# Moving three small pieces of work on VectorE and ScalarE in a gated MLP whose TensorE is nearly always busy

## The chip, the cores and the metric

The kernel runs on one core of a Trainium2 chip. The metric is the device time of one execution in microseconds (us); most executions of one kernel agree within 0.3%. Compared runs are fast ones (no lowered clock).

In the profile PE is TensorE (matmuls; PEld its weight loads), DVE is VectorE, ACT is ScalarE, POOL is GpSimd and SP issues most DMA transfers. L266 is line 266 of the kernel. Lines after 266 shift by some lines in the changed kernel: L270 becomes L276, L352 and L357 become L365 and L370, L320 becomes L333, L363 becomes L376, L347 becomes L360, L567 and L568 become L580 and L581.

## The reference

```python
# x: 16 x 256 x 512, w1: 512 x 4096, w2: 2048 x 512, all float32
h = x @ w1
gate, value = np.split(h, 2, axis=-1)
h = np.maximum(gate, 0) * value
return (h @ w2).astype(np.float32)
```

## The kernel before

The 4096 rows are done in four sets (s = 0 to 3) of 1024 rows. Both matrix products use a scheme with seven half-size products (P1 to P7) in place of eight, at the price of sums around them: sums of x ("x sums", S1 to S4), sums of weights (T1 to T4), and sums of the results in PSUM. X, Y and W are the PSUM tiles that the products accumulate into; "gating" is the step max(gate, 0) times value, which writes g; cc, pu and o are SBUF tiles for the sums around it.

The first product runs in 16 blocks per set. A block takes seven time slots of two matmuls (128x512), and each block is interleaved with its neighbours by the table SLOT. P4 of a block comes four slots after its P7; three slots after that P4 comes the next block's P7. So in DVE's queue a block's second-half gating (L270, behind P4) stands right ahead of the next block's cc (L266, behind P7):

```python
SLOT = {"P1": 0, "P5": 1, "P2": 3, "P6": 4, "P3": 5, "P7": 9, "P4": 13}   # PERIOD = 7

class Block:
    ...
    def P6(self):
        self.mm("P6", self.Y, False)                       # TensorE accumulates into PSUM tile Y
        nc.scalar.activation(self.u2, self.Y, COPY, scale=GS)
    def P3(self):
        self.mm("P3", self.W, False)
        ...
        nc.vector.scalar_tensor_tensor(out=self.c12, in0=self.W, ..., in1=self.u2, ...)       # L260, "cc<-W"
        nc.vector.scalar_tensor_tensor(out=self.g[:, self.jb, :TH], in0=self.X, ..., in1=self.c12, ...)  # L261
    def P7(self):
        self.mm("P7", self.Y, False)
        nc.vector.scalar_tensor_tensor(out=self.c22, in0=self.Y, ..., in1=self.p5, ...)       # L266, "cc<-Y"
    def P4(self):
        self.mm("P4", self.Y, False)                       # may start only when L266 has read Y
        nc.vector.scalar_tensor_tensor(out=self.g[:, self.jb, TH:], in0=self.Y, ..., in1=self.c22, ...)  # L270
```

The second product runs in four pairs (t = 0 to 3) per set, each with P1 to P7 of eight matmuls (128x256), spread by a list ORDER; its last P4 is interleaved with the next set's first block. "Looks" are checks of the weights' size: one is a square with a running sum on ACT, 128x1024, L179.

```python
ORDER = ("... P4 0, P5 2, P4 1, P6 2, P3 2, P7 2, P1 3, P4 2, P5 3, P2 3, P6 3, P3 3, P7 3, P4 3")

class Pair:
    ...
    def P6(self):
        nc.scalar.activation(self.pu[:, 1], self.Y, COPY, scale=1 / GS)
        for _ in range(2 if self.s else 1):
            some_look()
    def P4(self):
        nc.scalar.activation(self.o[:, 1, :DO // 2], self.Y, COPY, scale=1 / GS)
        ...
        if self.s == 0 and self.t < 3:
            some_look()
```

At the end of set 0 DVE makes the four x sums for set 1 itself, placed by step numbers in the second product's stream:

```python
for u in (84, 90, 93, 96):
    job(u, lambda sums=sums: next(sums))
...
advance(stream, 112 - TAIL - 10, jobs)
```

The x of set 1 reaches SBUF on a long road: POOL's queue issues a DMA that casts it to 16 bits in DRAM (`CASTS = {(0, 11): 1, ...}`: set 1, issued at block 11 of set 0), and eight transposing DMAs on SP's queue bring it in.

Of the kernel before, what the change touches and what calls it, by code (L numbers as in the profile page):

```python
# [96 lines left out]
def fast_way(ctx, tc, x2, w1, w2, out2, flag):  # L97
# [11 lines left out]
    _, J = w1.shape  # L109
    H, DO = w2.shape  # L110
    NS = T // (2 * TH)
    NJ = H // P
# [41 lines left out]
    def x_tiles():  # L154

        o = {n: xpool.tile([P, 2, TH], F16, name=f"x_{n}", tag=f"x_{n}")
             for n in ("A11", "A12", "A22", "S1", "S2", "S3", "S4")}
        o["A21"] = o["S3"]
        return o

    def sums_of(o, eng=nc.vector):
        for n, i0, i1, op in (("S1", "A21", "A22", ADD), ("S2", "S1", "A11", SUB), ("S4", "A12", "S2", SUB),
                              ("S3", "A11", "A21", SUB)):
            yield eng.tensor_tensor(o[n], o[i0], o[i1], op=op)  # L164
# [24 lines left out]
    def load_x(s, o):  # L189

        for h in range(2):
            for e in range(4):
                nc.sync.dma_start(out=o[f"A{h + 1}{e // 2 + 1}"][:, e % 2],
                                  in_=x16[s][h * TH:(h + 1) * TH, e * P:(e + 1) * P], transpose=True)

    def load_rows(s, i):

        t = halfs.tile([P, 8, P], F16, name="xh", tag="xh")
        nc.sync.dma_start(out=t.rearrange("p (b q) c -> p b (q c)", b=2),
                          in_=x16[s][i * 2 * P:(i + 1) * 2 * P].rearrange("(b p) d -> p b d", p=P))  # L200
        return t
# [24 lines left out]
    class Block:  # L226
# [25 lines left out]
        def P6(self):  # L252
            self.mm("P6", self.Y, False)
            nc.scalar.activation(self.u2, self.Y, COPY, scale=GS)  # L254
# [9 lines left out]
        def P7(self):  # L264
            self.mm("P7", self.Y, False)
            nc.vector.scalar_tensor_tensor(out=self.c22, in0=self.Y, scalar=GS, in1=self.p5, op0=MULT, op1=ADD)  # L266

        def P4(self):
            self.mm("P4", self.Y, False)
            nc.vector.scalar_tensor_tensor(out=self.g[:, self.jb, TH:], in0=self.Y, scalar=0.0,  # L270
                                           in1=self.c22, op0=MAX, op1=MULT)

    class Plain:

# [26 lines left out]
    class Pair:  # L301
# [43 lines left out]

        def P6(self):
            nc.scalar.activation(self.pu[:, 1], self.Y, COPY, scale=1 / GS)  # L347
            for _ in range(2 if self.s else 1):
                some_look()

        def P3(self):
# [10 lines left out]
        def P4(self):  # L362
            nc.scalar.activation(self.o[:, 1, :DO // 2], self.Y, COPY, scale=1 / GS)  # L363
            self.send(1, slice(0, DO // 2 if self.end else DO))
            if self.s == 0 and self.t < 3:  # L365
                some_look()

    ORDER = ("P1 0, P1 1, P2 0, P2 1, P1 2, P5 0, P2 2, P6 0, P3 0, P7 0, P5 1, P6 1, P3 1, P7 1, P4 0, P5 2, P4 1, "
# [5 lines left out]
    def mm2_stream(s, pairs):  # L374
        for step in (LAST_ORDER if s == NS - 1 else ORDER if s else FIRST_ORDER).split(", "):
            name, t = step.split()  # L376
            yield from pairs[int(t)].product(name)
# [3 lines left out]
    def advance(stream, n, todo={}):  # L381

        for _ in range(n):
            if stream is None:
                return
            at = stream_at[stream] = stream_at.get(stream, -1) + 1
            for job in todo.get(at, ()):
                job()
            next(stream, 0)
# [11 lines left out]
    def prepare(i):  # L401
        jb, n, _ = wl[i]
        copies.extend((i, c) for c in w1_ops(jb, n, ws.pop(i)))
# [51 lines left out]
    first_half, second_half = (xo["A11"], xo["A12"]), (xo["A21"], xo["A22"])  # L455
# [25 lines left out]
    sums = sums_of(xo)  # L481
# [15 lines left out]
    def some_look():  # L497
        if looks:
            looks.pop(0)()
# [43 lines left out]
    for s in range(NS):  # L543
        if s not in g_set:
            g_set[s] = gpool.tile([P, NJ, 2 * TH], F16, name="g", tag="g")
        g = g_set[s]
        first = NPLAIN if s == 0 else 0
        blocks = {jb: Block(xo, g, jb) for jb in range(first, NJ)}
        plan = {jb * PERIOD + at: (jb, n) for jb in blocks for n, at in SLOT.items()}
        stream = None  # L550
        last = NJ * PERIOD
        todo = 3
        for at in range(first * PERIOD, (NJ - 1) * PERIOD + 14):
            if at == last - 7:
                pairs = [Pair(s, g, t) for t in range(NB // 2)]
                stream = mm2_stream(s, pairs)
            if at in plan:
                jb, n = plan[at]
                if s == 0 and n == "P5" and jb % 2 == 0:
                    todo += 1  # L560
                    if todo < len(wl):
                        prepare(todo)
                    if 5 <= todo < 9:
                        n2 = ("B11", "T3", "B22", "B21")[todo - 5]
                        nc.gpsimd.dma_start(out=vop[n2], in_=w2_v[(0, 0, 1, 1)[todo - 5], (0, 1, 1, 0)[todo - 5]])
                if (s, n, jb) == (0, "P7", 13):
                    nc.gpsimd.tensor_tensor(vop["T1"], vop["T3"], vop["B11"], op=SUB)  # L567
                    nc.gpsimd.tensor_tensor(vop["T2"], vop["B22"], vop["T1"], op=SUB)  # L568
                if n == "P1" and jb == (14 if s == 0 else 2) and s + 1 < NS:
                    xo_next = x_tiles()  # L570
                    load_x(s + 1, xo_next)
                if n == "P1" and s and jb in (0, 3 if s == NS - 1 else 6):
                    wanted = [LOOKX[s, j] for j in range(NJ) if (s, j) in LOOKX]
                    rows += [load_rows(*r) for r in (wanted[3:] if jb else wanted[:3])]
                if n == "P1" and (s, jb) in CASTS:
                    cast_x(CASTS[s, jb])
                if s and n == "P3" and jb in SUMS and s + 1 < NS:
                    if jb == SUMS[0]:
                        sums = sums_of(xo_next, nc.gpsimd)
                    next(sums)  # L580
                getattr(blocks[jb], n)()  # L581
                if s == 0 and (n, jb) == ("P1", NPLAIN):
                    plain[1].value()
                if s == 0 and (n, jb) == ("P5", NPLAIN):
                    next(sums)
                    plain[1].gate(1)
                if n in ("P6", "P7"):
                    copy_some(1)
                if s == 0 and n == "P7" and jb % 2:
                    fetch(jb // 2 + 5, nc.sync)  # L590
                if n == "P6" and (s, jb) in LOOKX:
                    look_x(*LOOKX[s, jb])
            elif at >= last - 7:
                advance(stream, 2)
            else:
                advance(prev, 2)
        jobs = {}

        def job(at, *what):
            jobs.setdefault(at, []).extend(what)  # L600

        for t, at in enumerate(SUMS_AT if s else SUMS_FIRST):
            sums = sums_of(pairs[t].op)
            for u in at:
                job(u, lambda sums=sums: next(sums))
        if s == 0:
            for n2, i0, i1, at in (("T3", "B22", "T3", (46, 50)), ("T4", "B21", "T2", (57, 58))):
                for i, u in enumerate(at):
                    part = [vop[n][:, i * NJ // 4:(i + 1) * NJ // 4] for n in (n2, i0, i1)]
                    job(u, lambda part=part: nc.vector.tensor_tensor(*part, op=SUB))  # L610
            for i, u in enumerate((74, 78, 82, 83)):
                job(u, lambda i=i: plain_w_end(0, NPLAIN, i))
        if s + 1 < NS:
            xo = xo_next
            if s == 0:
                sums = sums_of(xo)
                for u in (84, 90, 93, 96):
                    job(u, lambda sums=sums: next(sums))
            looks = [lambda i=i: LOOK_JOBS[i]() for i in range(8 * s, 8 * s + 8)]
            advance(stream, 112 - TAIL - 10, jobs)  # L620
        else:
            verdict = []
            job(18, lambda: verdict.append(judge()))
            job(46, lambda: count(verdict[0]))
            job(78, lambda: verdict.append(nc.values_load(
                flag[0:1, 0:1], min_val=0, max_val=1, skip_runtime_bounds_check_because="a comparison wrote it")))
            job(90, lambda: tc.mark_branch_hint_location("general", "LikelyTaken", [ENG.PE, ENG.DVE, ENG.SP]))
            advance(stream, 112, jobs)
        prev = stream
# [29 lines left out]
```

## Time and profile before

| | before |
|---|---|
| time, median of 3 runs | 313.85 us (313.25 to 314.24) |
| span of the profiled run | 311.5 us, of which TensorE's last matmul ends at 306.7 |
| granted TensorE clock | 1.000 |

The head of the page of the kernel before: busy time by engine.

```profile
span 311.5 us, 5217 instructions
...
PE 302.7 (97%) x1870; PEld 182.8 (59%) x1870; DVE 231.2 (74%) x378; ACT 177.9 (57%) x350; POOL 153.9 (49%) x186
```

97% looks as if nothing were left. The record of a pipelined matmul overlaps the next one's, however: a 128x512 matmul is recorded with 379 ns and the next starts after 216 ns. The record hides a short stall. So I used the time between the starts of neighbouring matmuls, less 213.3 ns per 512 columns, and call the rest a gap. The 213.3 ns are an estimate: one column a cycle at 2.4 GHz, the highest clock that the Trainium skill's "TensorE: Matmul & The Clock Gate" gives in its first table; the 215 to 216 ns from start to start in this trace lie close to it. In undisturbed stretches the gap is 2 to 3 ns. Sums of gaps are taken beyond 2.5 ns each. They come to some 9 us in the kernel before, nearly 4 of them in the first 10 us.

The waits of PE (engine and tile that waited, what it waited for, us in total, times, longest):

```profile
...
PE Y L233 <- DVE cc L266: 0.7, 2, 0.5
PE Y L320 <- DVE o L357: 0.6, 1, 0.6
PE X L233 <- ACT Y L240: 0.2, 1, 0.2
...
```

This view shows the large stalls only. The gaps before P4 of all blocks after the first sum to 1.60 us in the trace, 0.37 us of it in one place (47 us); most are 35 to 46 ns and 5 to 18 ns in alternation. The view reports two of the P4 waits: the one at 47 us and one of 0.5 us before the first block's P4. Its wait for ACT (L240) is one at 18 us, which the change does not touch; the two stalls of 0.29 us behind L240 at the ends of sets 1 and 2, shown below, are not in it.

One ordinary block in the timeline of the kernel before (start, duration, engine, line, what):

```profile
103.77 0.69 DVE L260 SCALAR_TENSOR_TENSOR cc<-W,pu 128x512 f32<-128x512 f32 x1 [0.44 <-ACT pu L254]
104.49 0.69 DVE L261 SCALAR_TENSOR_TENSOR g<-X,cc 128x512 f16<-128x512 f32 x1
...
105.10 0.68 DVE L270 SCALAR_TENSOR_TENSOR g<-Y,cc 128x512 f16<-128x512 f32 x1
...
105.70 0.68 DVE L266 SCALAR_TENSOR_TENSOR cc<-Y,pu 128x512 f32<-128x512 f32 x1
105.96 0.59 PE L233 MATMUL W<-x_S_687,w_B_89 128*128 128x512 f16 x2
...
106.43 0.59 PE L233 MATMUL Y<-x_A_683,w_T_93 128*128 128x512 f16 x2
```

L270 (the previous block's second half) runs ahead of L266. L266 ends at 106.38 and the P4 matmul starts at 106.43; at pace it would have started at 106.39.

The end of set 0 in the timeline of the kernel before. The x sums are L164, the output sums L352 and L357:

```profile
82.98 0.69 DVE L164 TENSOR_TENSOR x_S_684<-x_S_686,x_A_683 128x1024 f16<-128x1024 f16 x1 [2.14 <-DMA x_A_683<-x_598]
...
85.04 0.68 DVE L164 TENSOR_TENSOR x_S_686<-x_A_681,x_S_686 128x1024 f16<-128x1024 f16 x1
...
85.64 0.42 DVE L352 SCALAR_TENSOR_TENSOR o<-W,pu_1002 128x256 f32<-128x256 f32 x1
...
85.97 0.42 DVE L357 SCALAR_TENSOR_TENSOR o<-Y,pu_1002 128x256 f32<-128x256 f32 x1
...
86.44 0.60 PE L320 MATMUL Y<-v_T_100,g 128*128 128x256 f16 x4 [0.57 <-DVE o L357]
```

DVE does four x sums, then the two output sums; P4 of the last pair starts 0.74 us late.

The end of set 1 in the same view. Two squares (L179) hold ACT, so its copy L240 is late, and P2 of the next set's first block (x_A_1145) with it, by 0.29 us:

```profile
158.58 1.06 ACT L179 ACTIVATE sq<-w_T_90 128x1024 f16<-128x1024 f16 x1
...
159.63 0.58 ACT L240 COPY Y<-X 128x512 f32<-128x512 f32 x1
...
160.26 0.59 PE L233 MATMUL X<-x_A_1145,w_B_88 128*128 128x512 f16 x2
```

### The profile page before, as it was taken

How to read it: one execution, taken by the hardware profiler on the slowest of the kernel's cores; microseconds unless marked ns; L12 is line 12 of the kernel's file. 1: busy time of each engine (PE TensorE's matmuls, PEld its weight loads, DVE VectorE, ACT ScalarE, POOL GpSimd, SP SyncE). 2: the span in 40 equal slices, each digit the busy share in tenths (PEclk: the TensorE clock that was granted, in tenths of full speed). 3: DMA queues.
4: the chain of work that ended last, by engine and by line, in shares of the span. 5: the costliest groups of instructions: out<-in, count | busy, mean ns of one | idle time of the engine just before them, and what ended most of it. 6: DMA issues, size and time to landing. Idle time of an engine off the chain costs nothing.

```text
span 311.5 us, 5217 instructions
## 1 busy us (share of the span) xinstructions
PE 302.7 (97%) x1870; PEld 182.8 (59%) x1870; DVE 231.2 (74%) x378; ACT 177.9 (57%) x350; POOL 153.9 (49%) x186
## 2 busy tenths in 40 slices
PE   7999999999999999999999999999999999999993
PEld 3934444588844444478864444458884444448883
DVE  1598888889758888887527888888536888888841
ACT  2688885445855555537675555545776555553230
POOL 2199999920058999400028889700007998700000
PEclk9999999999999999999999999999999999999999
DMA  7978695999784233000355400000335110000132
GB/s 241 354 221 258 183 222 76 202 205 151 214 243 102 70 69 67 2 0 36 136 171 117 117 1 3 0 0 9 128 107 164 37 34 1 0 3 0 69 140 66
DMA packets 37340, 32.87 MB, mean 106 GB/s; under 512 B 14400, under 2 KB 32320, under 8 KB 37184
## 3 DMA queue, kind: packets, MB, share of 16 engines
q1 hardware_dynamic: 31904, 25.70, 27.5%
q0 software_dynamic: 4352, 6.29, 11.8%
q10 hardware_dynamic: 1056, 0.52, 0.6%
q8 instruction: 15, 0.25, 0.3%
q14 instruction: 13, 0.11, 0.1%
HBM read 27.26 MB, written 12.58 MB: 128 GB/s over the span
## 4 chain that ended last, share of the span: by engine, by line
PE 69%; ACT 2%; issue 0%
PE Y L233 20%; PE X L233 13%; PE W L233 13%; PE Y L320 10%; PE X L320 7%; PE W L320 6%; ACT sq L179 1%; ACT Y L240 0%; ACT o L363 0%; ACT pu_1812 L347 0%; PE X L527 0%; ACT pu_2615 L347 0%
## 5 line engine op out<-in xcount | busy, mean ns | idle before, releaser
L170 POOL TENSOR_TENSOR fold<-xh 128x1024 f32<-128x1024 f16 x16 | 30.3, 1895 | 95.0 <-DMA xh<-x_696 35.0
L260 DVE SCALAR_TENSOR_TENSOR cc<-W,pu 128x512 f32<-128x512 f32 x62 | 42.9, 692 | 33.7 <-ACT pu L254 30.5
L254 ACT ACTIVATE pu<-Y 128x512 f32<-128x512 f32 x62 | 37.1, 598 | 34.9 <-PE Y L233 33.7
L240 ACT COPY Y<-X 128x512 f32<-128x512 f32 x62 | 35.4, 571 | 37.3 <-PE X L233 21.2
L173 POOL TENSOR_TENSOR fold<-fold 128x512 f32<-128x512 f32 (+2 forms) x96 | 51.9, 540 | 7.5
L320 PEld LDWEIGHTS <-w_stage 128*128 128x128 f16 x512 | 50.0, 98 | 5.9
L261 DVE SCALAR_TENSOR_TENSOR g<-X,cc 128x512 f16<-128x512 f32 x62 | 42.9, 692 | 2.3
L270 DVE SCALAR_TENSOR_TENSOR g<-Y,cc 128x512 f16<-128x512 f32 x62 | 42.3, 682 | 2.8 <-PE Y L233 2.8
L320 PEld LDWEIGHTS <-g 128*128 128x128 f16 x384 | 37.5, 98 | 9.0 <-issue 0.9
L266 DVE SCALAR_TENSOR_TENSOR cc<-Y,pu 128x512 f32<-128x512 f32 x62 | 42.3, 682 | 0.2
L247 ACT ACTIVATE pu<-W 128x512 f32<-128x512 f32 x62 | 37.1, 599 | 0.0
L164 DVE TENSOR_TENSOR w_stage<-g 128x1024 f16<-128x1024 f16 x32 | 21.4, 686 | 0.2
L233 PEld LDWEIGHTS <-w_T_93 128*128 128x128 f16 x124 | 12.0, 97 | 16.0 <-issue 4.2
L233 PEld LDWEIGHTS <-w_B_88 128*128 128x128 f16 x124 | 12.1, 98 | 15.0 <-issue 1.1
L233 PEld LDWEIGHTS <-w_B_89 128*128 128x128 f16 x124 | 12.1, 98 | 14.8 <-issue 0.3
L233 PEld LDWEIGHTS <-w_T_90 128*128 128x128 f16 x124 | 12.1, 98 | 14.7
L233 PEld LDWEIGHTS <-w_T_91 128*128 128x128 f16 x124 | 12.1, 98 | 14.7
L233 PEld LDWEIGHTS <-w_T_92 128*128 128x128 f16 x124 | 12.1, 98 | 13.8 <-issue 0.2
L233 PEld LDWEIGHTS <-w_B_87 128*128 128x128 f16 x124 | 11.9, 96 | 13.5
L320 PE MATMUL Y<-v_T_100,g 128*128 128x256 f16 x128 | 17.1, 273 | 0.6 <-DVE o L357 0.6
L320 PE MATMUL Y<-v_T_98,w_stage 128*128 128x256 f16 x128 | 16.8, 273 | 0.0
L320 PE MATMUL W<-v_B_96,w_stage 128*128 128x256 f16 x128 | 16.6, 273 | 0.0
(218 smaller groups left out, 565.4 us busy)
## 6 DMA issues: line engine op xcount, KB each, us to landing
out_dram<-o SPq DMA_DIRECT2D x30, 256.0 KB, 2.0
w_stage<-in_w_dram SPq DMA_DIRECT2D x14, 512.0 KB, 5.5
x_598<-in_x_dram POOLq DMA_DIRECT2D x1, 1024.0 KB, 10.1
x_653<-in_x_dram POOLq DMA_DIRECT2D x1, 1024.0 KB, 16.0
x_696<-in_x_dram POOLq DMA_DIRECT2D x1, 1024.0 KB, 19.8
xh<-x_653 SPq DMA_DIRECT2D x4, 256.0 KB, 3.4
xh<-x_598 SPq DMA_DIRECT2D x4, 256.0 KB, 3.9
x_1346<-in_x_dram POOLq DMA_DIRECT2D x1, 1024.0 KB, 7.5
```

What stands on the lines that cost most here:

```text
L164: yield eng.tensor_tensor(o[n], o[i0], o[i1], op=op)
L170: nc.gpsimd.tensor_tensor(fold, t, t, op=MULT)
L173: nc.gpsimd.tensor_tensor(fold[:, :, :m], fold[:, :, :m], fold[:, :, m:2 * m], op=ADD)
L233: nc.tensor.matmul(ps, wop[wn][:, b, self.jb * P:(self.jb + 1) * P], self.xo[xn][:, b, :], start=fresh and b == 0, stop=b == 1, skip_group ...
L240: nc.scalar.copy(out=self.Y, in_=self.X)
L247: nc.scalar.activation(self.p5, self.W, COPY, scale=GS)
L254: nc.scalar.activation(self.u2, self.Y, COPY, scale=GS)
L260: nc.vector.scalar_tensor_tensor(out=self.c12, in0=self.W, scalar=GS, in1=self.u2, op0=MULT, op1=ADD)
L261: nc.vector.scalar_tensor_tensor(out=self.g[:, self.jb, :TH], in0=self.X, scalar=0.0, in1=self.c12, op0=MAX, op1=MULT)
L266: nc.vector.scalar_tensor_tensor(out=self.c22, in0=self.Y, scalar=GS, in1=self.p5, op0=MULT, op1=ADD)
L270: nc.vector.scalar_tensor_tensor(out=self.g[:, self.jb, TH:], in0=self.Y, scalar=0.0, in1=self.c22, op0=MAX, op1=MULT)
L320: nc.tensor.matmul(ps, self.op[an][:, i], vop[wn][:, i], start=name in ("P1", "P5") and i == 0, stop=i == NJ // 2 - 1, skip_group_check=True)
```

## The change

Its intent is to take three kinds of small waits from TensorE by moving work in the queues of DVE and ACT. No instruction that works on data is added or removed. Piece 1 issues a block's second-half gating behind the next block's P7 sum. Piece 2 lets the last pair of sets 1 and 2 do no squares and puts one each behind P4 of pairs 0 and 1. Piece 3 puts two of the four x sums behind the last output sums.

```diff
         def P7(self):
             self.mm("P7", self.Y, False)
             nc.vector.scalar_tensor_tensor(out=self.c22, in0=self.Y, scalar=GS, in1=self.p5, op0=MULT, op1=ADD)
+            second_halves()
         def P4(self):
             self.mm("P4", self.Y, False)
+            later.append(self)
+            if self.jb == NJ - 1:
+                second_halves()
+
+        def second_half(self):
             nc.vector.scalar_tensor_tensor(out=self.g[:, self.jb, TH:], in0=self.Y, ...)
+    later = []
+    def second_halves():
+        while later:
+            later.pop(0).second_half()
 # ---- class Pair
         def P6(self):
             ...
-            for _ in range(2 if self.s else 1):
+            for _ in range(0 if self.s and self.t == 3 else 2 if self.s else 1):
                 some_look()
         def P4(self):
             ...
-            if self.s == 0 and self.t < 3:
+            if self.t < (2 if self.s else 3):
                 some_look()
 # ---- end of set 0
-                for u in (84, 90, 93, 96):
+                for u in (84, 90):
                     job(u, lambda sums=sums: next(sums))
             ...
             advance(stream, 112 - TAIL - 10, jobs)
+            if s == 0:
+                next(sums)
+                next(sums)
```

## The prediction

> **What bounds it.** The page gives PE 97% busy, and the chain of waits is mostly PE (69% of the span). The Trainium skill ("Perfetto Trace Analysis", Identifying the Most-Contended Engine) warns that matmul busy time is no measure of distance to the limit, so I took start-to-start times from the timeline. A 128x512 matmul starts every 215 to 216 ns, the 215.7 ns that the skill's "TensorE: Matmul & The Clock Gate" (Wait — 56ns, not 53.3ns?) states for a warm array. Against that pace PE loses some 9 us of 306.7: about 4 in the first 10 us, about 1.2 at 17 to 23 us, the rest in four small kinds of stalls. Then 4.9 us of tail. Only stalls after 17 us are touched.
>
> **Piece 1, gating order on DVE.** P4 of a block accumulates into Y once DVE has read Y for cc (L266). In the timeline (block at 103 to 107 us) DVE runs cc 103.77, g 104.49, second-half g 105.10, cc 105.70, ends 106.38, and P4 starts at 106.43: the start gap before P4 is 39 ns or 14 ns over pace in alternate blocks, and 371 ns once, at 47.2 us. Sum over all P4s, without the first block, 1.6 us. Moving the second-half g (0.68 us, 0.60 start to start) behind cc makes cc wait only for P7's end (about 105.3), so P4 has about 0.4 us to spare. Y is released some 1.3 us later; its next writer comes later still. The next cc (L260) waits for ACT's pu anyway (idle 0.42 us per block), so nothing moves there. At a set's end, the second pair's Y copy starts 0.3 to 0.4 us later but its P2 still has 0.2 us. Gain 1.6 us. The 644 ns stall at 22.3 us stays: no second half precedes that cc.
>
> **Piece 3, x sums.** At 84.4 and 85.0 us two x sums (0.69 us each) sit ahead of the last output sums; P4 of the last pair waits for o (L357), 0.74 us over pace (waits: 0.6 us). Behind them, o is ready at about 85.45, before PE asks at 85.70; the sums end by 86.9, and P3 and P7 need them later. Gain 0.7 us, once.
>
> **Piece 2, squares.** Last pair's two squares (1.17 us each) delay ACT's Y copy (L240) at 159.6 and 233.0 us: 0.29 us of PE each. Gain 0.58 us. But the moved squares follow P4 of pairs 0 and 1. Chaining ACT steps from 148.39 us (copy 0.28, square 1.17): P5's copy at 149.84, P4's at 150.14, square, then P6's u copy 151.6 to 152.0; P7 of pair 2 wants Y at 151.85. New stall about 0.18 us in sets 1 and 2: loss 0.36 us.
>
> **Sum.** 1.6 + 0.7 + 0.58 - 0.36 = 2.5 us, all on PE's chain. 313.85 - 2.5 = 311.35 us, range 310.5 to 312.6; faster by over 2% 0.01, within 2% 0.98, slower 0.01.
>
> **What shows it.** Right: P4's start gaps at pace after block 3; waits without "PE Y <- DVE o"; the transitions at about 158 and 231 us without PE waits; PE busy to about 304.2. The new stall: PE waits on ACT pu before P7 of pair 2.
>
> **What would make it wrong.** P7's end may bind cc later than I read, or L260 may slip behind the moved g; the delayed Y may stall the set's end; the 371 ns stall may be chance; a stall removed early may reappear where ACT or a transpose DMA limits next.

## The result

| | before | changed |
|---|---|---|
| time, median of 4 runs each | 313.83 us (313.25 to 314.24) | 311.09 us (310.94 to 311.45) |
| ratio | | 0.9912, 95% interval 0.9897 to 0.9928 |
| span of the profiled run | 311.5 us | 309.2 us |
| end of TensorE's last matmul | 306.7 us | 304.5 us |

The ratio and its interval come from the fast runs of both kernels in the same rounds; a ratio is not quite that of the medians quoted. Here the kernel is 0.9% faster.

The same parts of the profile after. The head of the page:

```profile
span 309.2 us, 5211 instructions
...
PE 301.5 (98%) x1870; PEld 183.2 (59%) x1870; DVE 236.4 (76%) x378; ACT 177.0 (57%) x350; POOL 153.7 (50%) x186
```

DVE's busy time rose by 5 us for the same 378 instructions. In the old order the records of L261, L270 and L266 overlap at two places by some 0.08 us each, and in the new order at one place per block, which over 62 blocks is about that much.

The waits of PE; the wait for o is gone and one of the two for L266 is left, the one before the first block's P4, which starts at 23.3 us:

```profile
...
PE Y L233 <- DVE cc L266: 0.5, 1, 0.5
PE X L233 <- ACT Y L240: 0.2, 1, 0.2
...
```

An ordinary block in the timeline:

```profile
104.11 0.69 DVE L266 SCALAR_TENSOR_TENSOR cc<-Y,pu 128x512 f32<-128x512 f32 x1
...
104.71 0.68 DVE L276 SCALAR_TENSOR_TENSOR g<-Y,cc 128x512 f16<-128x512 f32 x1
104.77 0.59 PE L233 MATMUL W<-x_S,w_B 128*128 128x512 f16 x2
...
105.20 0.59 PE L233 MATMUL Y<-x_A,w_T 128*128 128x512 f16 x2
```

L266 is now first and ends at 104.80, 0.40 us before P4 starts, at pace. The gaps before P4 after the first block fell from 1.60 us to 0.00 us.

The end of set 0, DVE's timeline and then PE's:

```profile
83.03 1.42 DVE L164 TENSOR_TENSOR x_S<-x_S,x_A 128x1024 f16<-128x1024 f16 x2 [2.57 <-DMA x_A<-x]
84.36 0.41 DVE L365 SCALAR_TENSOR_TENSOR o<-W,pu 128x256 f32<-128x256 f32 x1
84.70 0.41 DVE L370 SCALAR_TENSOR_TENSOR o<-Y,pu 128x256 f32<-128x256 f32 x1
85.03 1.28 DVE L164 TENSOR_TENSOR x_S<-x_A,x_S 128x1024 f16<-128x1024 f16 x2
...
85.32 0.60 PE L333 MATMUL Y<-v_T,g 128*128 128x256 f16 x4
```

The output sum ends at 85.11 and P4 starts at 85.32 without a gap. The two gaps of 0.29 us at the ends of sets 1 and 2 are gone as well. In the timeline of set 1, ACT is now free for its copy of X, and P2 starts at pace:

```profile
158.10 0.57 ACT L240 COPY Y<-X 128x512 f32<-128x512 f32 x1 [1.79 <-PE X L233]
...
158.76 0.59 PE L233 MATMUL X<-x_A,w_B 128*128 128x512 f16 x2
```

In their place stands one new gap in each of sets 1 and 2. ACT's timeline in set 1, then PE's:

```profile
149.02 1.05 ACT L179 ACTIVATE sq<-w_T 128x1024 f16<-128x1024 f16 x1
...
150.06 0.37 ACT L360 ACTIVATE pu<-Y 128x256 f32<-128x256 f32 x1
...
149.41 1.04 PE L333 MATMUL W<-v_B,w_stage 128*128 128x256 f16 x8
150.48 1.03 PE L333 MATMUL Y<-v_T,w_stage 128*128 128x256 f16 x8
```

Eight of these matmuls start within 0.87 us elsewhere; here 1.07 us pass between P3 (W) and P7 (Y), because ACT's copy of Y ended at 150.43 only. This gap of 0.20 us does not appear in the view of waits, since the overlapping record of the earlier matmul covers it.

Matching the two traces matmul by matmul from 10 us on, the gaps changed by -1.60 us before P4 of the blocks, -0.74 us at the end of set 0, -0.58 us at the ends of sets 1 and 2, and +0.40 us before P7 of pair 2, together -2.52 us. All other matmuls, most of them the same to 1 ns, add +0.19 us, and the first 10 us, where TensorE waits for DMAs, were 0.21 us slower in this profile. So TensorE's end came 2.13 us earlier. The span fell by 2.37 us, since what follows the last matmul took 4.62 us instead of 4.85. The median fell by 2.74 us.

### The profile page after: what moved, and what is told of

Same layout as the page of the kernel before. It is cut to its first block, busy times and chain, and to the rows that moved or that the text cites. A ratio compares the mean times of both kernels' runs of the same rounds, so it can differ in the third digit from the quotient of the medians.

```text
span 309.2 us, 5211 instructions
## 1 busy us (share of the span) xinstructions
PE 301.5 (98%) x1870; PEld 183.2 (59%) x1870; DVE 236.4 (76%) x378; ACT 177.0 (57%) x350; POOL 153.7 (50%) x186
## 4 chain that ended last, share of the span: by engine, by line
PE 93%; DVE 2%; DMA 2%; issue 1%; SPq 0%; ACT 0%; DVEq 0%
PE Y L233 26%; PE X L233 17%; PE W L233 17%; PE Y L333 14%; PE X L333 9%; PE W L333 9%; DMA x_A<-in_x_dram 2%; DVE x_S L164 1%; PE X L448 1%; DVE g L308 1%; PE X L301 1%; PE W L301 1%; PE W L448 0%; PE Y L150 0%; DVE x_S L450 0%
## 5 line engine op out<-in xcount | busy, mean ns | idle before, releaser
L233 PEld LDWEIGHTS <-w_T 128*128 128x128 f16 x496 | 48.5, 98 | 57.5 <-issue 1.0
L233 PE MATMUL X<-x_A,w_B 128*128 128x512 f16 x248 | 73.7, 379 | 0.2 <-ACT Y L240 0.2
L233 PE MATMUL Y<-x_S,w_T 128*128 128x512 f16 x248 | 73.8, 379 | 0.0
L233 PEld LDWEIGHTS <-w_B 128*128 128x128 f16 x372 | 36.4, 98 | 42.6 <-issue 0.8
L260 DVE SCALAR_TENSOR_TENSOR cc<-W,pu 128x512 f32<-128x512 f32 x62 | 42.8, 691 | 19.5 <-ACT pu L254 19.5
L266 DVE SCALAR_TENSOR_TENSOR cc<-Y,pu 128x512 f32<-128x512 f32 x62 | 42.8, 691 | 7.2 <-PE Y L233 0.7
L261 DVE SCALAR_TENSOR_TENSOR g<-X,cc 128x512 f16<-128x512 f32 x62 | 42.9, 691 | 2.3
L276 DVE SCALAR_TENSOR_TENSOR g<-Y,cc 128x512 f16<-128x512 f32 x62 | 42.2, 681 | 1.8 <-PE Y L233 1.8
L233 PE MATMUL Y<-x_A,w_T 128*128 128x512 f16 x124 | 36.9, 379 | 0.5 <-DVE cc L266 0.5
L233 PE MATMUL W<-x_S,w_T 128*128 128x512 f16 x124 | 36.9, 379 | 0.0
L233 PE MATMUL W<-x_S,w_B 128*128 128x512 f16 x124 | 36.9, 379 | 0.0
L333 PE MATMUL Y<-v_T,w_stage 128*128 128x256 f16 x256 | 33.2, 272 | 0.1
L333 PE MATMUL X<-v_B,g 128*128 128x256 f16 x256 | 31.9, 273 | 0.0
L365 DVE SCALAR_TENSOR_TENSOR o<-W,pu 128x256 f32<-128x256 f32 x16 | 6.7, 422 | 18.7 <-PE W L333 18.7
```

The lines of the kernel that those rows point to most:

```text
L233: nc.tensor.matmul(ps, wop[wn][:, b, self.jb * P:(self.jb + 1) * P], self.xo[xn][:, b, :], start=fresh and b == 0, stop=b == 1, skip_group ...
L260: nc.vector.scalar_tensor_tensor(out=self.c12, in0=self.W, scalar=GS, in1=self.u2, op0=MULT, op1=ADD)
L266: nc.vector.scalar_tensor_tensor(out=self.c22, in0=self.Y, scalar=GS, in1=self.p5, op0=MULT, op1=ADD)
L333: nc.tensor.matmul(ps, self.op[an][:, i], vop[wn][:, i], start=name in ("P1", "P5") and i == 0, stop=i == NJ // 2 - 1, skip_group_check=True)
```

## The experiments

All outputs are right. Ratios and intervals are against the kernel before in the same rounds. "Gap at the end of set 0" is the one before P4 of the last pair.

### Piece 1 alone

```diff
 the diff above, without the edits of class Pair and of the end of set 0
```

> The kernel before with piece 1 alone (second half of the gating behind the next P7 sum). My theory: cc no longer queues behind the second half on DVE, so every P4 after the first block starts at pace. PE's end comes 1.6 us earlier, time about 312.2 us; excess gaps before P4 (other than the 0.64 us of the first block) fall from 1.6 us to about 0; the 0.74 us at the set-0 end and the two 0.29 us at the ends of sets 1 and 2 stay. Rival (the 371 ns stall at 47 us is chance and the 14 to 46 ns gaps are PE's own semaphore cost): gaps of 14 to 46 ns stay, time within 0.4 us of before.

Measured: 312.87 us (311.81 to 313.60) against 313.59, ratio 0.9974 (0.9956 to 0.9992). In its profile the gaps before P4 are gone (0.00 us), so the rival about chance and semaphores falls. But the time fell by 0.7 us, not the 1.6 expected, and the spread is wide. The profile, of the fastest of the six runs, shows where a little of it went: the gap at the end of set 0 grew from 0.74 to 0.90 us. The sums there start when the transposed x lands. TensorE asked 0.55 us earlier than in the kernel before, and x landed only 0.40 us earlier.

### Piece 2 alone

```diff
 the two edits of class Pair only
```

> The kernel before with piece 2 alone (no squares in the last pair, one each after P4 of pairs 0 and 1). My theory: the two 0.29 us stalls before the second P2 of the next set go, and two new stalls of 0.20 us come before P7 of pair 2, so only 0.2 us is gained, about 313.6 us. Rival (the 0.20 us stalls of the changed kernel come from the earlier pieces, for instance from DVE having shifted): no stall before P7 of pair 2 here, gain 0.6 us.

Measured: 313.50 us (313.14 to 314.24) against 313.59, ratio 0.9991 (0.9975 to 1.0007). The profile has the two new gaps of 0.20 us before P7 of pair 2 and lacks the two of 0.29 us, as expected. Piece 2 by itself is worth about 0.2 us in gaps and nothing that the times can tell from zero. By chance this profile began its matmuls of the first set 1.9 us late, and it has no gap at the end of set 0: a hint that this gap depends on TensorE's distance to something with its own clock.

### Piece 3 alone

```diff
 the edits at the end of set 0 only
```

> The kernel before with piece 3 alone (two x sums behind the last output sums). My theory: the 0.74 us stall before the last pair's P4 at about 85.5 us goes and nothing comes in its place: gain 0.7 us, about 313.1 us. Rival (P4 there waits for the transposes' landing through the first x sum, which is not moved): stall stays above 0.4 us.

Measured: 312.76 us (312.54 to 313.07), ratio 0.9967 (0.9952 to 0.9983). The gap is 0.00 us. The gain is as expected or a little more.

### The kernel before, profiled again

No edit.

> The unchanged kernel before, profiled a second time. If the 371 ns stall before P4 at about 47 us is fixed by the program, it is there again with about that size; if it is chance, it is absent or elsewhere. The alternating 39 and 14 ns gaps before P4 should be there again either way under my theory.

Measured, one run: 313.28 us. The stall before P4 at 47 us is back with 0.365 us, and all gaps before P4 sum to nearly the same, 1.58 us, so both belong to the program.

### Pieces 1 and 3

```diff
 the diff above, without the edits of class Pair
```

> Pieces 1 and 3 without piece 2. Theory: the gain of piece 1 in the first set (0.56 us) is swallowed at the set's end when the x sums stay ahead of the output sums, because those sums start when the transposed x lands, which does not move; with the sums moved behind it is kept. So the two together give more than their sum: PE's end near 304.7 us, time about 311.3 us. Rival (the pieces simply add, and gate_only's 0.7 us is what piece 1 is worth): 313.6 - 0.8 - 1.0, about 311.8 us. Both: no large gap at 85 us, two of 0.29 us at the ends of sets 1 and 2.

Measured: 311.51 us (311.17 to 311.62) against 313.46, ratio 0.9926 (0.9901 to 0.9952). The two pieces together save 1.95 us by the medians, where singly they saved 0.72 and 0.83: they give more than their sum, though the intervals overlap too much to prove this by time alone. PE ended at 304.84. I had expected no large gap at 85 us; there was one of 0.22 us. The two of 0.29 us at the ends of sets 1 and 2 were there as expected.

### Piece 1 alone, with the cast of x one block earlier

```diff
 piece 1, and
-    CASTS = {(0, 11): 1, (0, 13): 0, (0, 14): 2, (1, 8): 3}
+    CASTS = {(0, 10): 1, (0, 13): 0, (0, 14): 2, (1, 8): 3}
```

> Piece 1 alone, and the cast of x for set 1 issued one block earlier, which in GpSimd's queue is ahead of one more group of weight sums (about 6 us earlier). Theory: the 0.90 us stall before the last pair's P4 of set 0 is the landing of the transposed x plus four sums; landed some us earlier, the sums run in time and the stall is gone without moving them: time about 0.9 us or more below gate_only, near 311.9 us, and a narrower spread. Rival (the stall is DVE's own backlog of sums, whatever lands): stall stays at 0.7 us or more.

Measured: 311.36 us (310.82 to 311.75), ratio 0.9927 (0.9902 to 0.9953). The four x sums are still ahead of the output sums, but they start at 80.45 instead of 82.58 us, and the gap at the end of set 0 is 0.00. DVE's timeline of this kernel:

```profile
80.45 1.42 DVE L164 TENSOR_TENSOR x_S<-x_S,x_A 128x1024 f16<-128x1024 f16 x2 [0.26 <-issue]
81.90 1.29 DVE L164 TENSOR_TENSOR x_S<-x_A,x_S 128x1024 f16<-128x1024 f16 x2
83.56 0.42 DVE L365 SCALAR_TENSOR_TENSOR o<-W,pu 128x256 f32<-128x256 f32 x1 [0.36 <-PE W L333]
```

The first sum no longer waits for a DMA, and the output sum waits for TensorE instead of TensorE for it. The cast was issued 5.8 us earlier than with piece 1 alone (48.47 instead of 54.28 us), but the last transposed x landed only 2.1 us earlier (80.37 instead of 82.50); what took the rest was not tested. The rival (DVE's own backlog) falls.

### The squares behind pairs 0 and 2

```diff
-            if self.t < (2 if self.s else 3):
+            if self.t in (0, 2) if self.s else self.t < 3:
                 some_look()
```

> The changed kernel with the single squares of sets 1 and 2 behind P4 of pairs 0 and 2 instead of 0 and 1. Theory: the 0.20 us stall before P7 of pair 2 comes of two squares in a row of copies (P4 of pair 0, P4 of pair 1) that make ACT late for P6's copy; with one of them after P4 of pair 2 there is no stall anywhere in the pairs: two times 0.2 us less, about 310.7 us. Rival (one square already makes it late, or the later one stalls the end of the set): 0.1 to 0.3 us gaps remain in sets 1 and 2 and the time is as that of the changed kernel.

Measured: 311.15 us (310.76 to 311.30), ratio 0.9913 (0.9888 to 0.9939). The two gaps of 0.20 us are gone and nothing took their place in the pairs, so the mechanism is as stated. The time missed the expected 310.7: the profile, whose first set is the same program as the changed kernel's, has 0.38 us at the end of set 0. DVE's timeline, then PE's:

```profile
83.48 1.42 DVE L164 TENSOR_TENSOR x_S<-x_S,x_A 128x1024 f16<-128x1024 f16 x2 [3.11 <-DMA x_A<-x]
84.81 0.42 DVE L365 SCALAR_TENSOR_TENSOR o<-W,pu 128x256 f32<-128x256 f32 x1
85.15 0.41 DVE L370 SCALAR_TENSOR_TENSOR o<-Y,pu 128x256 f32<-128x256 f32 x1
...
85.61 0.60 PE L333 MATMUL Y<-v_T,g 128*128 128x256 f16 x4 [0.22 <-DVE o L370]
```

The same instructions in the same order as in the changed kernel, 0.45 us later, because x landed later.

### The old order on DVE from block 8 on

```diff
         def P4(self):
             later.append(self)
-            if self.jb == NJ - 1:
+            if self.jb == NJ - 1 or self.jb >= 8:
                 second_halves()
```

> The changed kernel with the old DVE order (second half ahead of the next cc) from block 8 of each set on. Theory: gaps before P4 at pace (2 to 3 ns) up to block 8, and the old 46 and 5 or 39 and 14 ns pattern from block 9 on, with the 0.37 us one at about 47 us back, for it is block 10: some 1.0 us over pace in all. Rival (the gaps come from somewhere else that the change shifted, such as Y's release): no switch at block 8.

Measured, one run: 311.76 us. In set 1 the gaps before P4 are 2 to 4 ns for blocks 0 to 8 and 45, 7, 41, 9, 40, 9, 13 ns for blocks 9 to 15; sets 2 and 3 switch at the same block, and the stall at 47 us is back (0.33 us). In all 0.90 us. The order of these two instructions in one block makes the gap of that block. DVE's timeline at the switch, new order first (L266, L276), then old:

```profile
113.60 0.69 DVE L266 SCALAR_TENSOR_TENSOR cc<-Y,pu 128x512 f32<-128x512 f32 x1
114.21 0.68 DVE L276 SCALAR_TENSOR_TENSOR g<-Y,cc 128x512 f16<-128x512 f32 x1
...
116.42 0.68 DVE L276 SCALAR_TENSOR_TENSOR g<-Y,cc 128x512 f16<-128x512 f32 x1
117.02 0.68 DVE L266 SCALAR_TENSOR_TENSOR cc<-Y,pu 128x512 f32<-128x512 f32 x1
```

### The changed kernel with the earlier cast

```diff
-    CASTS = {(0, 11): 1, ...}
+    CASTS = {(0, 10): 1, ...}
```

> The changed kernel with the cast of x for set 1 issued one block earlier, nothing else. Theory: at the end of set 0 the changed kernel still depends on when the transposed x lands (gaps of 0, 0.22 and 0.38 us at 85 us in three profiles of the same program up to there); landed early, the gap is 0 in every profile and the mean gain over the changed kernel is 0.1 to 0.3 us, with a narrower spread. Rival (the spread is measuring noise): no difference.

Measured: 311.20 us (311.03 to 311.38), ratio 0.9921 (0.9899 to 0.9944). No gap at the end of set 0. A gain over the changed kernel (311.09, in other rounds) is not to be seen, and the spread (0.35 against 0.51 us) says little with so few runs: the gain that I expected in the time was not shown.

### The plain block's gating behind the next cc

The first two blocks of the first set use a plain scheme, and DVE gates the second of them ahead of block 2's cc. That is the 0.63 us gap before P4 at 23.3 us that the change left.

```diff
                 if s == 0 and (n, jb) == ("P5", NPLAIN):
                     next(sums)
+                if s == 0 and (n, jb) == ("P7", NPLAIN):
                     plain[1].gate(1)
```

> The changed kernel with the second plain block's gating put behind block 2's cc on DVE, the same re-ordering as piece 1, in the one place that the change left: P4 of block 2 waits 0.63 us there for a cc behind that gating. Theory: the gap before P4 of block 2 falls from 0.63 us to under 0.1 us and the rest is as in the changed kernel: about 0.6 us less, unless the earlier PE meets the landing of x at 85 us, which can take back up to as much. Rival (the late x sums before it, slowed to 1.2 to 1.6 us, hold DVE anyway): gap stays above 0.4 us.

Measured: 311.35 us (311.11 to 311.68), ratio 0.9928 (0.9905 to 0.9951): no gain. The gap fell from 0.63 to 0.04 us as expected. Two others opened: 0.26 us at the end of set 0, where x landed at its own time, and 0.24 us before the matmul at 64.9 us, where P5 of the second product waits for its first sum S1. The latter, in the timelines of POOL and DVE of this kernel:

```profile
60.24 4.06 POOL L581 TENSOR_TENSOR v_T<-v_B,v_T 128x2048 f16<-128x2048 f16 x1
...
63.46 1.38 DVE L164 TENSOR_TENSOR w_stage<-g 128x1024 f16<-128x1024 f16 x1
```

The sum is recorded with 1.38 us instead of the usual 0.69. In the kernel before it ran after POOL's 128x2048 sum had ended (start 64.39, POOL's end 64.07) and took 0.69 us. In all nine profiles where it started before that end, it ended 0.55 us after it (0.545 to 0.554); in the five where it started later it took 0.69. The Trainium skill ("SBUF — State Buffer", Who interferes with whom) says that a VectorE instruction with two SBUF inputs contends with a GpSimd instruction that reads SBUF; the trace agrees, though no run here varied this alone.

### All repairs together

```diff
 the earlier cast, the squares behind pairs 0 and 2, the plain block's gating behind the next cc
```

> The changed kernel with all three repairs: squares behind P4 of pairs 0 and 2, the plain block's gating behind block 2's cc, the cast one block earlier. Theory: the gains add, for the cast has taken away the landing that could take them back: 0.4 + 0.6 + 0.1 to 0.3 us below the changed kernel, about 309.9 us; no gap above 0.1 us after 20 us.

Measured: 310.78 us (310.41 to 311.28), ratio 0.9909 (0.9886 to 0.9932). Against the changed kernel with the early cast, in the same rounds, that is 0.42 us less by the medians; I had expected about 1 us more than the changed kernel gives. A gap of 0.44 us before the matmul at 62.2 us swallowed most of the 0.6. The waits of PE in this kernel name it:

```profile
PE X L333 <- DMA v_B<-in_w_dram: 0.3, 1, 0.3
```

The last load of w2 is issued behind the cast in POOL's queue now and lands at 62.1 us instead of 59.8 in the changed kernel, just when a TensorE that runs 0.6 us earlier asks for it. It was issued only 0.7 us later (54.29 instead of 53.57), so most of the delay came on its way, for a reason that no run here tests.

### The same without piece 3

```diff
 the four x sums back at steps 84, 90, 93, 96
```

> The same with piece 3 undone: all four x sums ahead of the last output sums again. Theory: piece 3 was only a way round the late landing; with an early cast the sums finish in time where they stood, so this is as fast as with piece 3, within 0.2 us, and shows no gap at the end of set 0. Rival (the order on DVE matters by itself): 0.5 us or more slower, with a gap before the last pair's P4.

Measured: 310.77 us (310.46 to 311.10), ratio 0.9910 (0.9887 to 0.9932), and no gap at the end of set 0. With x landed early, piece 3 is worth nothing that these runs show. The rival (the order matters by itself) falls.

## Why the prediction was right

**The sum.** Predicted 311.35 us, measured 311.09; a gain of 2.5 us predicted, 2.74 measured. The four terms summed to 2.52 us in the trace, so the sum was right where it can be checked. That the time agrees so closely is in part luck: TensorE's end was expected near 304.2 us and came at 304.5 (0.2 us of that from the slower start of that profile), and 0.24 us of the gain in span came after the last matmul, where nothing was forecast.

**Piece 1, 1.6 us of gaps.** Right in mechanism and size: 1.60 us. The block experiment shows the mechanism, as the gaps switch with the order of two instructions. The side effects that I ruled out stayed away: L260 still waits for ACT, though for 0.20 us instead of 0.42, as the moved instruction takes that room; the later release of Y stalled nothing. What I did not see: this gain is not secure as time. Alone, piece 1 gave 0.7 us by the medians.

**Piece 3, 0.7 us "once".** The size was right in the profile, but the reason was incomplete. I read "two sums ahead of the output sums" as the cause and named the landing of x as something that might limit elsewhere. It is one part of the cause; when x lands is the other. Fourteen profiles give one rule. Here "landed" is the last transposed x of set 1 in the trace, "asked" the time at which P4 would start at pace (us):

| kernel | landed | P4 asked | asked less landed | P4 started | started less landed |
|---|---|---|---|---|---|
| four sums ahead | | | | | |
| before | 82.90 | 85.70 | 2.81 | 86.44 | 3.55 |
| before again | 83.00 | 85.83 | 2.82 | 86.55 | 3.55 |
| piece 1 | 82.50 | 85.15 | 2.65 | 86.05 | 3.55 |
| piece 2 | 83.80 | 87.46 | 3.66 | 87.47 | no wait |
| piece 1, early cast | 80.37 | 85.05 | 4.68 | 85.05 | no wait |
| repairs without piece 3 | 80.58 | 85.23 | 4.66 | 85.23 | no wait |
| two sums ahead | | | | | |
| piece 3 | 82.80 | 85.89 | 3.08 | 85.89 | no wait |
| changed | 82.95 | 85.32 | 2.37 | 85.32 | no wait |
| old order from block 8 | 82.69 | 85.75 | 3.05 | 85.75 | no wait |
| pieces 1 and 3 | 83.25 | 85.24 | 1.99 | 85.47 | 2.22 |
| squares behind 0 and 2 | 83.40 | 85.23 | 1.83 | 85.61 | 2.22 |
| plain gating late | 83.07 | 85.03 | 1.96 | 85.29 | 2.22 |
| changed, early cast | 80.87 | 85.21 | 4.34 | 85.21 | no wait |
| all repairs | 80.70 | 85.36 | 4.65 | 85.36 | no wait |

With four sums ahead P4 cannot start sooner than 3.55 us after the landing, with two not sooner than 2.22. Every profile obeys it. Piece 3 shortens the road behind the landing by 1.33 us. The changed kernel's profile met the limit with 0.15 us to spare; two others with the same first set up to there, and one that runs it earlier, did not. So my "0.7 us, once" holds for a landing near 82.9 us, and that it showed whole in this profile was luck; when x lands later, part of TensorE's gains in set 0 is lost. Among the programs with the late cast the landing varied by 0.9 us in nine profiles (82.50 to 83.40); the tenth, of piece 2, landed at 83.80 after a start that was 1.9 us late. It does not follow TensorE: pieces 1 and 3 asked 0.46 us earlier than the kernel before and x landed 0.35 us later.

**Piece 2, +0.58 and -0.36 us.** Right: +0.58 and -0.40 in the gaps; alone it gave nothing that the times can tell from zero. Chaining the measured steps of ACT gave the new gap as 0.18 us; it was 0.20.

**What stays open.** Piece 1 alone varied from 311.8 to 313.6 us. Only the run at 311.8 was profiled. A later landing in the other runs may be part of it, and with the early cast the runs lay between 310.8 and 311.8, but none of the longer runs was traced; by the 3.55 us rule the whole 1.8 us would need a landing near 84.3 us, later than any profile shows (83.80), so the cause of this spread stays open. That the kernel with all repairs beats the changed one is not shown: it was 0.42 us faster than the changed one with the early cast in the same rounds, but the ratios against the kernel before are 0.9909 and, for the changed kernel, 0.9912, and the two were not measured in one set of rounds.

## What to carry to other kernels

When TensorE is 97% busy, measure stalls from start to start of its instructions: stalls of up to 0.29 us lay under overlapping records here, and those before P4 of 61 blocks made 1.6 us. Put on each queue first what TensorE will ask for next, and what merely frees a buffer after it; but chain the measured steps of the queue to see where the moved work lands, since a square moved off one wait made another. And ask of each wait whether it hangs on the engine's order or on an arrival with its own clock, such as a DMA landing: against an arrival, finishing earlier elsewhere gains nothing, and the levers are to shorten the work behind it, as piece 3 did by 1.33 us, or to issue it earlier, behind which the next arrival may stand.

## What the Trainium skill lacked or had wrong

- "Perfetto Trace Analysis" (Identifying the Most-Contended Engine) warns against matmul busy time; it does not say that recorded waits too are hidden by the overlap. Here the waits of PE name 0.7 us for cc in the kernel before, while the gaps before P4 sum to 2.2 us with the first block's 0.64, and stalls of 0.29 and 0.20 us are not listed at all.
- "SBUF — State Buffer" (Who interferes with whom) has the contention of VectorE and GpSimd right. It does not say how it looks in a profile: as busy time of the instruction (up to 1.38 us recorded for 0.69), not as a wait, ending 0.55 us after GpSimd's instruction in nine profiles.
- No page that I read tells how much the landing of transposing DMAs varies from run to run: the last of eight landed between 82.5 and 83.4 us in nine profiles of programs that issue them alike.
